# A two-layer mLSTM/gMLP trunk on one core: the opening phase in a new order, with x transposed first and the gates last

## The chip, the cores and the metric

The kernel runs on one core of a Trainium2 chip. Its time is the device time of one execution in microseconds (us). A core has TensorE (PE, matrix products; PEld is its weight load), VectorE (DVE), ScalarE (ACT) and GpSimd (POOL), and SyncE (SP), which here only issues loads and stores. SBUF is the memory on the core, PSUM the eight banks into which TensorE writes.

## The reference

Input x is 512 rows of 1024 numbers; c is one row of 1024. There are two layers. Each has a token mixer (layer 0: mLSTM, layer 1: a chunked gMLP) and a channel MLP. Around each stands adaLN: shift, scale and gate are computed from c.

```python
mod = silu(c) @ ada_w[i] + ada_b[i]
sh1, sc1, g1, sh2, sc2, g2 = split(mod, 6)
h = rmsnorm(x, norm_g[i, 0]) * (1.0 + sc1) + sh1
y = mixer(h)                                  # layer 0: mLSTM
x = x + g1 * rmsnorm(y, norm_g[i, 1])
h = rmsnorm(x, norm_g[i, 2]) * (1.0 + sc2) + sh2
x = x + g2 * rmsnorm(square(relu(h @ ffn_w1[i])) @ ffn_w2[i], norm_g[i, 3])
```

The mLSTM mixer projects h with one matrix of 3088 columns: q (512 columns, 8 heads of 64), k (512), v (1024), o (1024), input gates (8) and forget gates (8). From the gates come, per head, running sums and running maxima along the sequence, which give decay masks for the scores q k^T in chunks of 128 rows and the state that goes from chunk to chunk. All is float32.

## The kernel before

Products of float32 matrices are done as three matmuls of rounded parts (`mm3`): each operand is split into a rounded half (hi) and the remainder (lo), and hi*hi, hi*lo and lo*hi are added in one PSUM bank. `conv` makes the two halves of a weight block: ScalarE rounds, VectorE subtracts. Weight blocks of 1 MB go through a ring of five buffers (`raw`). Each engine works through its own queue in order. In the opening, which is pinned, the order on an engine is that of the program; behind the line `pinned[0] = False` a planner orders the instructions.

The layer-0 adaLN columns are computed in eight steps, one for each 128 of the 1024 features, since step k of the projections needs shift and scale of features 128k to 128k+127. For one step, `ada_load` brings 1 MB of `ada_w` (two loads of 512 KB, shift and scale, in pieces of 512 bytes). `ada_init` lets ScalarE multiply two of its eight row groups by silu(c) into two accumulators, `ada_acc` adds the other six on VectorE, `ada_merge` adds the accumulators on POOL, `ada_tr` transposes the result on TensorE, and `ada_fin` sums along the row on VectorE and makes the two columns in three small operations.

The opening of `mlstm` (lines 531 to 645) goes like this. SP issues the load of c, the adaLN block 0, the four tiles of x (512 KB each), then four small loads of gate weights in pieces of 32 bytes, the gate biases, and from there one q block (256 KB) and one adaLN block for each step. ScalarE issues four small loads of packed vectors from its own queue, before its first computing instruction. x is normalised per row: ScalarE squares and sums, POOL takes the power -1/2, VectorE scales. In the loop over k (8 steps) TensorE transposes four blocks of normalised x into PSUM, ScalarE applies scale and shift (`feed`), rounds, and POOL subtracts; POOL also subtracts for the q weights. Then TensorE does 15 matmuls of 512 columns: three for the gates and twelve for q, into five open banks. The transposes for step k+2 stand behind the matmuls of step k. After the loop k is projected, four blocks of 24 matmuls; its weights come as two loads of 1 MB. At the same time VectorE, ScalarE and TensorE compute the chain from the gates: tanh, log-sigmoid (a long polynomial on 8 partitions), running sums, running maxima, exponentials. These go through DRAM (`dm`) and come back as broadcast loads, from which POOL and ScalarE make the masks. Then v (8 units of 24 matmuls), and then scores, masks, state and the o units are interleaved by a list.

```python
        for step in "s0 k0 o0 m0 t0 o1 s1 k1 o2 m1 t1 o3 s2 k2 o4 m2 t2 g0 o5 s3 g1 o6 m3 g2 o7 g3".split():
```

Here s0 are the scores of chunk 0, o0 the first o unit, m0 the product with the masks. `prep.step()` works at the adaLN of the next part, beside the projections. PSUM is divided: five banks for `bank()`, two for `bank2()`, one for `bank3()`.

Of the kernel before, what the change touches and what calls it, by code (L numbers as in the profile page):

```python
# [8 lines left out]
F32 = mybir.dt.float32  # L9
# [24 lines left out]
def trunk(ctx: ExitStack, tc: tile.TileContext, x, c, norm_g, ada_w, ada_b, ffn_w1, ffn_w2,  # L34
# [77 lines left out]
    pool.memset(mhalf, -0.5)  # L112

# [417 lines left out]
    def mlstm(h, prep, after):  # L531
        w = a_w_in[0]
        h = HT()
        raws = [ada_load(0, 0, 1, 0)]
# [5 lines left out]
        wgs = w.rearrange("(k p) f -> p k f", p=P)  # L540
        wg = []
        for i in range(2):
            t = A(shape=(P, 4, P))
            pool.memset(t, 0.0)
            ld.dma_start(t[:, :, 0:8], wgs[:, 4 * i:4 * i + 4, 3072:3080])
            ld.dma_start(t[:, :, 32:40], wgs[:, 4 * i:4 * i + 4, 3080:3088])
# [3 lines left out]
        ld.dma_start(bcol[0:8, :], a_b_if[0, 0:8].rearrange("(p a) -> p a", a=1))  # L550
        ld.dma_start(bcol[32:40, :], a_b_if[0, 8:16].rearrange("(p a) -> p a", a=1))

        accs_ = {}
        qr = [None] * KC

        def load_q(k):
            qr[k] = A()
            ld.dma_start(qr[k], w[k * P:(k + 1) * P, 0:S])

        def ada_start(k):  # L560
            accs_[k] = R().rearrange("p (c i f) -> p c (i f)", c=2, i=2)
            ada_init(raws[k], accs_[k])

        load_q(0)
        raws.append(ada_load(0, 0, 1, 1))
        load_q(1)
        ada_start(0)
        ada_acc(raws[0], accs_[0], range(6))
        pt = bank2()
        for i in range(2):  # L570
            pe.transpose(out=pt[:, i * P:(i + 1) * P], in_=pk[:, i, :], identity=ident)
        aps = ada_tr(accs_[0])
        xn = []
        for t in range(NT):
            s = meansq(xt[t], D)
            v = small(1)
            pool.tensor_scalar_add(v, s, EPS)
            r = small(1)
            pool.tensor_tensor(out=r, in0=v, in1=mhalf[:, 0:1], op=ALU.pow)
            xs = [A(), A()]  # L580
            for s in range(2):
                dve.tensor_scalar_mul(xs[s], xt[t][:, s * S:(s + 1) * S], r)
            xn.append(xs)
            if t == 2:
                dve.tensor_copy(cols, pt[:, 0:2 * P].rearrange("p (a b) -> p a b", a=2))
                ab = [ada_fin(aps, 0, 0, 1, 0, 0)]
        accs = [bank() for _ in range(5)]
        qw = [None] * KC

        def xT(k):  # L590
            ps = bank2()
            for t in range(NT):
                pe.transpose(out=ps[:, t * P:(t + 1) * P],
                             in_=xn[t][k // 4][:, (k % 4) * P:(k % 4 + 1) * P], identity=ident)
            return ps

        def q_hi(k):
            qw[k] = A(F32R), A(F32R)
            act.copy(qw[k][0], qr[k])

        def q_lo(k):
            pool.tensor_sub(qw[k][1], qr[k], f32(qw[k][0]))

        def feed(k, ps, eng):
            full = T()
            act.activation(full, ps, AF.Identity, scale=ab[k][0], bias=ab[k][1])
            hh, hl = h(k, slice(0, S))
            act.copy(hh, full)
            eng.tensor_sub(hl, full, f32(hh))

        wgc = [conv(wg[i], lo_eng=pool) for i in range(2)]
        q_hi(0)
        q_lo(0)
        feed(0, xT(0), dve)
        pool.tensor_scalar_mul(bcol, bcol, 1.0 / CAP)
        ada_start(1)
        ada_acc(raws[1], accs_[1], range(6))
        raws.append(ada_load(0, 0, 1, 2))
        load_q(2)
        ada_start(2)  # L620
        aps = ada_tr(accs_[1])
        xps = xT(1)
        for k in range(KC):
            if k + 2 < KC:
                ada_acc(raws[k + 2], accs_[k + 2], range(6))
            if k + 1 < KC:
                ab.append(ada_fin(aps, 0, 0, 1, 0, k + 1))
            if k + 3 < KC:
                raws.append(ada_load(0, 0, 1, k + 3))
                load_q(k + 3)  # L630
                ada_start(k + 3)
            if k + 2 < KC:
                ada_merge(accs_[k + 2])
            if k + 1 < KC:
                feed(k + 1, xps, pool)
                q_hi(k + 1)
                q_lo(k + 1)
            hh, hl = h(k, slice(0, S))
# [521 lines left out]
```

## Time and profile before

| | |
|---|---|
| three timed runs | 1268.44, 1270.19, 1271.1 us; median 1270.19 |
| the profiled execution | 1269.99 us, of which the span is 1268.2 |
| PE | 1210.4 us busy, 95% of the span |
| DVE | 848.0, 67% |
| ACT | 619.5, 49% |
| POOL | 129.2, 10% |
| loads and stores | 174.24 MB, mean 137 GB/s |

The span runs from the first to the last instruction. A busy time is the time in which an engine has an instruction running. PE is almost always busy, so what ends the idle time of PE is what counts. The profile names every instruction by its engine and its tiles: `ps`, `pt`, `pa` are PSUM banks, `hhi` and `hlo` the halves of h, `whi` and `wlo` those of a weight block, `raw` a loaded block, `a` a general buffer, `r` an adaLN accumulator, `t` a short-lived buffer, `s` a small column.

### The profile page before, as it was taken

Reading aid. Unit: us, or ns where it says so; the run is one execution under the profiler, and the core shown is the slowest. Engines: PE = TensorE matmul, PEld = TensorE weight load, DVE = VectorE, ACT = ScalarE, POOL = GpSimd, SP = SyncE. Lnnn points to the kernel's source line nnn. Section 1 sums busy time; section 2 is a strip of 40 time slices with the busy share of each in tenths; the row PEclk is TensorE's granted clock in tenths of the full one; section 3 lists DMA queues with packets and bytes.
Section 4 is the critical chain, followed back from the end, with each engine's and each line's share of the span. In section 5 each row is a group of like instructions: output and inputs, shape, how many; then the busy total and the mean of one; then the engine's idle time right before and its main releaser. Section 6 shows DMA issues by size and latency. Waiting matters only on the chain.

```text
span 1268.2 us, 15234 instructions
## 1 busy us (share of the span) xinstructions
PE 1210.4 (95%) x5705; PEld 986.0 (78%) x5705; DVE 848.0 (67%) x1360; ACT 619.5 (49%) x1107; POOL 129.2 (10%) x158
## 2 busy tenths in 40 slices
PE   2999998999999999999899999999999999999997
PEld 1678777888787887778678788888798888887886
DVE  5897677573967869866666756532747758668545
ACT  4545535285555545553653644322664554545432
POOL 4601211010000000010110023300100000000000
PEclk9999999999999999999999999999999999999999
DMA  9957942433354363365256644332443332331401
GB/s 262 307 185 193 264 127 89 141 125 103 105 166 133 101 198 111 93 213 176 97 154 212 206 119 137 128 108 67 133 133 108 109 125 66 122 111 51 148 1 67
DMA packets 165722, 174.24 MB, mean 137 GB/s; under 512 B 6152, under 2 KB 121080, under 8 KB 165648
## 3 DMA queue, kind: packets, MB, share of 16 engines
q1 hardware_dynamic: 165408, 173.17, 44.0%
q8 instruction: 45, 0.74, 0.2%
q14 instruction: 29, 0.24, 0.1%
q10 hardware_dynamic: 240, 0.09, 0.0%
HBM read 171.11 MB, written 2.14 MB: 137 GB/s over the span
## 4 chain that ended last, share of the span: by engine, by line
PE 70%; DVE 11%; DMA 7%; ACT 5%; issue 2%; POOL 2%; SPq 2%; DVEq 0%; POOLq 0%; ACTq 0%
PE ps L50 49%; PE pt L50 21%; DMA raw<-in_ada_w 5%; DVE wlo L50 3%; DVE a L50 3%; DVE r L50 2%; SPq L50 2%; ACT whi L50 2%; ACT j L50 2%; POOL s L50 1%; ACT t L50 1%; DMA a<-in_b_ws 1%; DVE x L50 1%; DMA raw<-in_a_w_in 1%; DVE s L50 1%
## 5 line engine op out<-in xcount | busy, mean ns | idle before, releaser
L50 DVE TENSOR_TENSOR wlo<-raw,whi 128x1024 fp32r<-128x1024 f32 x232 | 284.8, 1232 | 203.0 <-ACT whi L50 197.5
L50 PE MATMUL ps<-whi,a 128*128 128x512 f32 x1312 | 418.9, 394 | 0.5 <-DVE a L50 0.3
L50 ACT CAST whi<-raw 128x1024 fp32r<-128x1024 f32 x232 | 242.4, 1051 | 309.6 <-PE ps L50 220.4
L50 PEld LDWEIGHTS ps<-whi,a 128*128 128x128 f32 x1312 | 246.4, 188 | 61.8 <-DVE a L50 5.4
L50 PE MATMUL ps<-wlo,a 128*128 128x512 f32 x656 | 256.7, 392 | 0.0
L50 DVE SCALAR_TENSOR_TENSOR r<-raw,cact,r 128x256 f32<-128x256 f32 (+1 forms) x256 | 143.7, 599 | 26.1 <-ACT r L50 13.3
L50 PE MATMUL pt<-hhi,whi 128*128 128x512 f32 x384 | 150.7, 392 | 2.2 <-ACT t L50 1.3
L50 PE MATMUL pt<-hhi,wlo 128*128 128x512 f32 x384 | 149.9, 391 | 1.5 <-DVE wlo L50 1.5
L50 PE MATMUL pt<-hlo,whi 128*128 128x512 f32 x384 | 149.5, 389 | 0.0
L50 PEld LDWEIGHTS ps<-wlo,a 128*128 128x128 f32 x656 | 123.6, 188 | 25.3 <-DVE wlo L50 1.2
L50 PE MATMUL ps<-hlo,whi 128*128 128x512 f32 (+1 forms) x360 | 127.7, 355 | 2.4 <-POOL hlo L50 2.4
L50 PE MATMUL ps<-hhi,whi 128*128 128x512 f32 (+1 forms) x360 | 129.1, 359 | 0.3 <-ACT whi L50 0.3
L50 PE MATMUL ps<-hhi,wlo 128*128 128x512 f32 (+1 forms) x360 | 127.5, 354 | 0.7 <-DVE wlo L50 0.7
L50 DVE TENSOR_TENSOR a<-a,a 128x512 fp32r<-128x512 f32 (+2 forms) x162 | 105.1, 685 | 32.0 <-ACT a L50 31.7
L50 PE MATMUL ps<-wlo,hhi 128*128 128x512 f32 x256 | 102.6, 401 | 6.0 <-DVE wlo L50 5.8
L50 PE MATMUL ps<-whi,hhi 128*128 128x512 f32 x256 | 102.7, 402 | 2.1 <-ACT whi L50 2.1
L50 PE MATMUL ps<-whi,hlo 128*128 128x512 f32 x256 | 101.5, 396 | 0.0
L50 ACT CAST a<-a 128x512 fp32r<-128x512 f32 x108 | 63.2, 616 | 53.9 <-POOL a L50 41.8
L50 POOL TENSOR_TENSOR s<-s,mhalf 128x1 f32<-128x1 f32 (+1 forms) x40 | 32.4, 811 | 548.9 <-DVE s L50 541.6
L50 PEld LDWEIGHTS pt<-hhi,whi 128*128 128x128 f32 x384 | 72.1, 188 | 19.0 <-ACT whi L50 2.5
L50 PEld LDWEIGHTS pt<-hhi,wlo 128*128 128x128 f32 x384 | 72.1, 188 | 18.6 <-DVE wlo L50 3.7
L50 PEld LDWEIGHTS pt<-hlo,whi 128*128 128x128 f32 x384 | 72.1, 188 | 14.7
(128 smaller groups left out, 1376.8 us busy)
## 6 DMA issues: line engine op xcount, KB each, us to landing
raw<-in_ffn_w SPq DMA_DIRECT2D x64, 1024.0 KB, 5.1
raw<-in_ada_w SPq DMA_DIRECT2D x64, 512.0 KB, 5.5
raw<-in_ada_w SPq DMA_DIRECT2D x16, 1024.0 KB, 5.1
raw<-in_b_w_in SPq DMA_DIRECT2D x16, 1024.0 KB
raw<-in_a_w_in SPq DMA_DIRECT2D x10, 1024.0 KB, 10.2
raw<-in_b_w_out SPq DMA_DIRECT2D x8, 1024.0 KB, 5.0
raw<-in_a_w_out SPq DMA_DIRECT2D x4, 1024.0 KB, 5.0
x<-in_x SPq DMA_DIRECT2D x4, 512.0 KB, 6.5
```

The source lines that it names most:

```text
L50: r = f(*a, **k)
```

## The change

The opening of `mlstm` is written anew; the rest of the kernel, but for the small column function, stays.

SP now loads x first, and then for each step the adaLN block, the q block and 384 of the 512 columns of k, 192 KB. Steps 0 to 2 are loaded at once, step k+3 behind the matmuls of step k. x is normalised, transposed by TensorE (32 blocks) and copied by ScalarE and VectorE into two of the five `raw` buffers before the loop. ScalarE starts one accumulator from one row group (`init`), VectorE adds seven (`sums`), and the sum over partitions is a product with a column of ones on TensorE (`total`), which gives a column at once. The column operations become two (`ada_cols`), as 1 is added to all scale biases once. The remainders of weights and of h are made by VectorE, no longer by POOL. The loop does 21 matmuls per step, for q (four banks) and three quarters of k (three banks). The gates come behind the loop, 24 matmuls; their weights come by one load in the third step and are spread by POOL. The last quarter of k is one block of 24 matmuls.

```diff
-        ab = cp.tile([P, 4], F32, tag="ab", name=nm("ab"), bufs=16)
-        dve.tensor_scalar(ab[:, 2:3], s[:, 1:2], abcol(l, vc, k), 1.0, ALU.add, ALU.add)
+        return ada_cols(s, l, vs, vc, ng, k)
+
+    def ada_cols(s, l, vs, vc, ng, k):
+
+        ab = cp.tile([P, 2], F32, tag="ab", name=nm("ab"), bufs=16)
+        dve.tensor_scalar(ab[:, 1:2], s[:, 1:2], abcol(l, vc, k), ngcol(l, ng, k), ALU.add, ALU.mult)
         dve.tensor_add(ab[:, 0:1], s[:, 0:1], abcol(l, vs, k))
-        dve.tensor_mul(ab[:, 1:2], ab[:, 2:3], ngcol(l, ng, k))
...
+        QK = S + 3 * P
+        def load(k):
+            raws[k] = ada_load(0, 0, 1, k)
+            raw = A(), A()[:, 0:QK - S]
+            ld.dma_start(raw[0], w[k * P:(k + 1) * P, 0:S])
+            ld.dma_start(raw[1], w[k * P:(k + 1) * P, S:QK])
+            qk[k] = [raw]
...
+        def init(k):
+            accs_[k] = R()[:, 0:2 * P]
+            act.activation(accs_[k], flat(k, KC - 1), AF.Copy, scale=cact[:, KC - 1:KC])
+        def sums(k):
+            a = accs_[k]
+            for j in range(KC - 1):
+                dve.scalar_tensor_tensor(out=a, in0=flat(k, j), scalar=cact[:, j:j + 1], in1=a,
+                                         op0=ALU.mult, op1=ALU.add)
+        def total(k):
+            ps = bank3()
+            for i in range(2):
+                pe.matmul(ps[:, i:i + 1], lhsT=accs_[k][:, i * P:(i + 1) * P], rhs=one, start=True, stop=True)
+            return ps
...
+        for k in range(3):
+            load(k)
+        xT = [rp.tile([P, 4, S], F32, tag="raw", name=nm("raw")) for _ in range(2)]
...
+        x_stat(0)
+        x_stat(1)
+        x_turn(0)
+        x_stat(2)
+        x_turn(1)
+        x_out(0)
+        x_stat(3)
+        x_turn(2)
+        x_out(1)
...
+        x_turn(3)
+        x_out(2)
+        init(0)
...
+        x_out(3)
+        sums(0)
+        sp0 = total(0)
+        ab = [ada_cols(sp0, 0, 0, 1, 0, 0)]
...
+        qk_hi(0)
+        full = feed_hi(0)
+        qk_lo(0)
+        feed_lo(0, full)
+        init(1)
+        sums(1)
+        qk_hi(1)
+        accs = [bank() for _ in range(5)] + [bank2() for _ in range(2)]
...
+        for k in range(KC):
+            main(k, range(5))
+            if k + 1 < KC:
+                sp1 = total(k + 1)
+            main(k, range(5, 7))
+            if k + 3 < KC:
+                load(k + 3)
...
+            if k + 2 < KC:
+                init(k + 2)
+            if k + 1 < KC:
+                ab.append(ada_cols(sp1, 0, 0, 1, 0, k + 1))
+                qk_lo(k + 1)
+                full = feed_hi(k + 1)
+                feed_lo(k + 1, full)
+            if k + 2 < KC:
+                qk_hi(k + 2)
+                sums(k + 2)
+        wgc = [conv(wg[i]) for i in range(2)]
+        gps = bank3()
...
+            mm3(gps, wgc[k // 4][0][:, k % 4], wgc[k // 4][1][:, k % 4], hh, hl, k == 0, k == KC - 1)
...
-        for f0 in (512, 768):
-            for blk in (kblk if f0 == 512 else w_cols(w, f0)):
-                ps = bank()
-                proj_fm(ps, blk, h, slice(0, S))
-                kk = A()
-                act.activation(kk, ps, AF.Copy, scale=DK ** -0.5)
-                kT.append(kk)
+        raw = rp.tile([P, KC, P], F32, tag="raw", name=nm("raw"))
+        ld.dma_start(raw, w[:, QK:2 * S].rearrange("(k p) f -> p k f", p=P))
+        ps = bank()
+        proj_fm(ps, conv(raw), h, slice(0, S))
+        for f in range(4):
+            kk = A()
+            act.activation(kk, accs[4 + f] if f < 3 else ps, AF.Copy, scale=DK ** -0.5)
+            kT.append(kk)
```

## Rows read from the trace of the kernel before

**Rows 1.** Busy time by stretch: from:to and length in us, then for each engine busy us and its number of instructions, the granted clock, the share of the DMA engines and GB/s. The stretches are the opening, the loop over k, the k projections, the v projections and the start of the attention part.

```profile
0.00:28.00 28.00, 4.39 (x15) 2.78 (x16) 15.65 (x33) 11.61 (x21) 12.76 (x29) 1.00 0.91 256
28.00:67.20 39.20, 36.31 (x159) 27.25 (x158) 32.74 (x64) 22.46 (x38) 24.05 (x21) 1.00 0.94 277
67.20:89.00 21.80, 21.80 (x98) 18.06 (x97) 20.55 (x27) 7.66 (x12) 0.00 (x0) 1.00 0.61 205
89.00:136.50 47.50, 47.28 (x216) 37.98 (x215) 33.82 (x70) 25.14 (x68) 8.24 (x24) 1.00 0.76 215
136.50:200.00 63.50, 57.58 (x374) 46.20 (x373) 48.25 (x148) 28.24 (x80) 11.17 (x8) 0.97 0.60 176
```

**Rows 2.** Timeline of the opening: load issues by SP and ACT and ScalarE's first computing instruction (start us, duration us, engine, operation, tiles, count), and behind them, from the view of the loads of x, the time from issue to landing.

```profile
1.27 1.03 SPq L50 DMA_DIRECT2D raw<-in_ada_w  x2
2.34 2.70 SPq L50 DMA_DIRECT2D x<-in_x  x4
2.80 0.55 ACTq L50 DMA_DIRECT2D a<-in_norm_g  x1
5.28 0.52 ACTq L50 DMA_DIRECT2D a<-in_a_hnorm_g  x1
7.17 0.38 SPq L50 DMA_DIRECT2D a<-in_a_w_in  x1
8.92 0.32 ACTq L50 DMA_DIRECT2D a<-in_b_b_in  x1
9.35 0.91 ACT L50 ACTIVATE r<-raw,cact 128x256 f32<-128x256 f32 x2 [6.38 <-DMA x<-in_x]
12.82 0.37 SPq L50 DMA_DIRECT2D a<-in_a_w_in  x1
...
DMA to landing us min/median/max: 6.5/6.5/6.5
```

**Rows 3.** Timeline: the steps by which x is made ready, and the first products of adaLN on VectorE.

```profile
9.89 2.46 DVE L50 SCALAR_TENSOR_TENSOR r<-raw,cact,r 128x256 f32<-128x256 f32 x6 [5.77 <-DMA a<-in_a_hnorm_g]
10.16 1.04 ACT L50 ACTIVATE j<-x 128x1024 bf16<-128x1024 f32 x1
13.57 0.57 POOL L50 TENSOR_TENSOR s<-s,mhalf 128x1 f32<-128x1 f32 x1
14.18 0.88 DVE L50 TENSOR_SCALAR a<-x,s 128x512 f32<-128x512 f32 x2 [1.82 <-POOL s L50]
37.83 0.60 PE L50 MATMUL pt<-ident,a 128*128 128x128 f32 x4
```

**Rows 4.** Timeline: the first projection, and single steps of the loop over k and their like elsewhere (h's remainder on VectorE, h scaled and rounded on ScalarE, TensorE waiting for POOL, the adaLN products beside POOL's work and without it, a column operation, f32 matmuls).

```profile
22.91 0.69 DVE L50 TENSOR_TENSOR hlo<-t,hhi 128x512 fp32r<-128x512 f32 x1 [0.63 <-ACT hhi L50]
28.03 0.78 PE L50 MATMUL ps<-hhi,whi 128*128 128x512 f32 x1
41.20 0.78 ACT L50 ACTIVATE t<-pt,ab 128x512 f32<-128x512 f32 x1 [1.87 <-DVE ab L50]
42.01 0.62 ACT L50 CAST hhi<-t 128x512 fp32r<-128x512 f32 x1
44.26 0.51 PE L50 MATMUL ps<-hlo,whi 128*128 128x512 f32 x1 [1.07 <-POOL hlo L50]
45.64 5.09 DVE L50 SCALAR_TENSOR_TENSOR r<-raw,cact,r 128x256 f32<-128x256 f32 x6
93.05 1.04 PE L50 MATMUL pt<-triu,s 128*8 128x128 f32 x8
144.02 0.15 DVE L50 TENSOR_TENSOR ab<-s,cols 128x1 f32<-128x1 f32 x1
147.08 3.25 DVE L50 SCALAR_TENSOR_TENSOR r<-raw,cact,r 128x256 f32<-128x256 f32 x8
```

**Rows 5.** Busy time by stretch, columns as in rows 1: TensorE's first matmuls, a stretch of the loop with a wait for POOL, and the matmuls behind the first wait for o weights.

```profile
28.00:32.00 4.00, 4.00 (x11) 3.16 (x10) 3.61 (x12) 2.15 (x5) 0.73 (x1) 1.00 1.17 305
42.70:46.00 3.30, 2.00 (x7) 1.14 (x7) 3.26 (x7) 1.54 (x4) 3.29 (x3) 1.00 1.18 300
141.40:144.60 3.20, 3.20 (x9) 2.42 (x9) 3.20 (x7) 3.18 (x7) 0.00 (x0) 0.50 0.70 205
```

**Rows 6.** Timeline of PE: the first matmul of the k projections, and the first of the v projections, 96 matmuls later.

```profile
67.18 0.39 PE L50 MATMUL ps<-hhi,whi 128*128 128x512 f32 x1
88.94 0.39 PE L50 MATMUL ps<-whi,hhi 128*128 128x512 f32 x1
```

**Rows 7.** Timeline of the chain behind the gates: tanh, the copy of the packed rows, the exponentials of the masks, the load of o weights behind the broadcast loads, and the first product of a mask with the scores.

```profile
64.42 0.68 ACT L50 ACTIVATE a<-ps,bcol 40x512 f32<-40x512 f32 x1
110.16 0.56 DVE L50 COPY a<-pt 128x384 f32<-128x384 f32 x1 [0.81 <-PE pt L50]
122.45 4.80 ACT L50 ACTIVATE a<-a,a 128x128 f32<-128x128 f32 x16 [2.27 <-POOL a L50]
122.97 1.41 SPq L50 DMA_DIRECT2D raw<-in_a_w_in  x1
144.09 0.68 DVE L50 TENSOR_TENSOR a<-a,ps 128x512 f32<-128x512 f32 x1
```

**Rows 8.** Timeline of PE in the first o block: matmuls that waited for o weights (in brackets the idle time and what ended it).

```profile
139.34 0.50 PE L50 MATMUL ps<-whi,hhi 128*128 128x512 f32 x1 [0.87 <-ACT whi L50]
147.22 0.50 PE L50 MATMUL ps<-wlo,hhi 128*128 128x512 f32 x1 [0.61 <-DVE wlo L50]
```

More of the change, by code (lines that the diff above doesn't have):

```diff
@@ L112, in trunk @@
     pool.memset(mhalf, -0.5)
+    one = cp.tile([P, 1], F32, name="one")
+    pool.memset(one, 1.0)
     ck = cp.tile([8, P], F32, name="ck")
@@ new lines, in qk_lo, with flat @@
+        def qk_lo(k):
+            raw, hi = qk[k]
+            lo = wp.tile([P, QK], F32R, tag="wlo", name=nm("wlo"))
+            dve.tensor_sub(lo[:, 0:S], raw[0], f32(hi[:, 0:S]))
+            dve.tensor_sub(lo[:, S:QK], raw[1], f32(hi[:, S:QK]))
+            qk[k].append(lo)
+        def flat(k, j):
+            return raws[k][:, j].rearrange("p a b -> p (a b)")
+        def init(k):
+            accs_[k] = R()[:, 0:2 * P]
+            act.activation(accs_[k], flat(k, KC - 1), AF.Copy, scale=cact[:, KC - 1:KC])
@@ new lines, in mlstm, with x_stat, x_turn @@
+        xT = [rp.tile([P, 4, S], F32, tag="raw", name=nm("raw")) for _ in range(2)]
+        rs, xps = {}, {}
+        def x_stat(t):
+            v = small(1)
+            pool.tensor_scalar_add(v, meansq(xt[t], D), EPS)
+            rs[t] = small(1)
+            pool.tensor_tensor(out=rs[t], in0=v, in1=mhalf[:, 0:1], op=ALU.pow)
+        def x_turn(t):
+            for s in range(2):
+                xn = A()
+                dve.tensor_scalar_mul(xn, xt[t][:, s * S:(s + 1) * S], rs[t])
+                ps = bank()
+                for j in range(4):
+                    pe.transpose(out=ps[:, j * P:(j + 1) * P], in_=xn[:, j * P:(j + 1) * P], identity=ident)
+                xps[t, s] = ps
@@ new lines, in x_out @@
+        def x_out(t):
+            for s, f in ((0, act.copy), (1, dve.tensor_copy)):
+                f(xT[s][:, :, t * P:(t + 1) * P], xps[t, s].rearrange("p (a b) -> p a b", a=4))
+        x_stat(0)
[7 more added lines that the diff above has]
+        x_out(1)
+        pt = bank2()
+        for i in range(2):
+            pe.transpose(out=pt[:, i * P:(i + 1) * P], in_=pk[:, i, :], identity=ident)
+        x_turn(3)
@@ new lines, in mlstm, with feed_hi @@
+        x_out(2)
+        init(0)
+        dve.tensor_copy(cols, pt[:, 0:2 * P].rearrange("p (a b) -> p a b", a=2))
+        scales = cols[:, 1, 0:96].rearrange("p (a b) -> p a b", b=KC)[:, 1::3, :]
+        dve.tensor_scalar_add(scales, scales, 1.0)
+        x_out(3)
+        sums(0)
+        sp0 = total(0)
+        ab = [ada_cols(sp0, 0, 0, 1, 0, 0)]
+        def feed_hi(k):
+            full = T()
+            act.activation(full, xT[k // 4][:, k % 4], AF.Identity, scale=ab[k][0], bias=ab[k][1])
+            act.copy(h(k, slice(0, S))[0], full)
+            return full
@@ new lines, in feed_lo, with main @@
+        def feed_lo(k, full):
+            hh, hl = h(k, slice(0, S))
+            dve.tensor_sub(hl, full, f32(hh))
+        qk_hi(0)
[6 more added lines that the diff above has]
+        accs = [bank() for _ in range(5)] + [bank2() for _ in range(2)]
+        def main(k, fs):
+            hh, hl = h(k, slice(0, S))
+            for f in fs:
+                cs = slice(f * P, (f + 1) * P)
+                mm3(accs[f], qk[k][1][:, cs], qk[k][2][:, cs], hh, hl, k == 0, k == KC - 1)
@@ L541, in mlstm @@
+        wgr = A()[:, 0:KC * 2 * NH].rearrange("p (k f) -> p k f", k=KC)
         wg = []
@@ L565, in mlstm @@
[L565 to L602, printed above, removed]
@@ L647, in mlstm @@
+        wgc = [conv(wg[i]) for i in range(2)]
+        gps = bank3()
+        for k in range(KC):
+            hh, hl = h(k, slice(0, S))
+            mm3(gps, wgc[k // 4][0][:, k % 4], wgc[k // 4][1][:, k % 4], hh, hl, k == 0, k == KC - 1)
         pinned[0] = False
```

77 lines of the change are left out of this document (19 added, 58 removed).

## The prediction, made before the changed kernel was timed

> **What bounds the kernel now.** I read the busy time by stage first. The reader should see one bound nearly everywhere: from the first projections on, TensorE is busy 36.3 of 39.2 us, then all of 21.8, then 47.3 of 47.5 [rows 1]. The exception is the opening. In the first 28 us TensorE works 4.4 us, while loads move 256 GB/s, and the attention part that starts at 136.5 us loses about 6 us more [rows 1]. So the change can win only where TensorE waits now: before the first projection at 28.03 [rows 4], inside the loop over k, and indirectly in the attention part, whose start depends on the forget-gate chain.
>
> Next I read the timeline of the opening [rows 2], to see what the first projection waits for: loads, then ScalarE, then VectorE. After that comes one turn of the loop with the durations of its steps [rows 3, 4], then the chain behind the gates [rows 7] and the waits of the first o block [rows 8].
>
> All sums go against the profiled execution: 1269.99 us, of which the span is 1268.2. That is 0.2 us under the median of the three timed runs, 1270.19.
>
> **Part 1, up to the first projection.** ScalarE is the gate. It issues four small loads from its own queue, and its first computing instruction waits behind them: the fourth goes out at 8.92 and takes 0.32, and at 9.35 ScalarE begins [rows 2]. The issue times tell why. Counted from the load of c, the tenth load goes out at 5.28, the eleventh at 7.17 and the twelfth at 8.92. The fourth (x, issued 2.34, landing after 6.5) lands at 8.84 [rows 2]. I read it so: about eight loads are under way at once, and the next waits for the oldest. By the same reading the load at 12.82 waited for the last tile of x, so tiles of x land (12.82 - 8.84) / 3 = 1.3 us apart and halves of the adaLN block 1.9 apart [rows 2].
>
> In the new order the SP queue begins c, four of x, two of adaLN, q, k. The first lands as the adaLN half did, at about 5.3 [rows 2]; x is complete at 5.3 + 3 x 1.3 = 9.2, the adaLN halves follow at 11.1 and 13.0, q and k by some 14.6. Which places ScalarE's four loads get is not shown. If they come right behind c, ScalarE is free by 8; if each alternates with an SP load that waits as well, the fourth is the seventeenth and waits for the ninth, until 14.6. I take the middle, the thirteenth or fourteenth place, behind x's last tile or adaLN's first half: about 10.
>
> From there, the chain by rows: four statistics (1.04 each, put at 1.2 with the reading of the sum) with a copy of 0.6 between them, so that the fourth ends some 5.2 us after the start; 1.05 for POOL's add and power (0.57 for the power, the rest an estimate); 0.9 for two scalings; 0.6 for four transposes; VectorE's copies, cols and scales about 1.6; seven products of adaLN at 0.41, 2.9; ones-column sums 0.4; two column operations 0.3; scaling and rounding of h 0.7 + 0.62 [rows 3, 4]. With hops this is 14.2 until the rounded half of h is there and 15.0 until the remainder is. So the first matmul comes at 24.2, and they run freely from 25.0, against 28.03 before: 3.0 us earlier. Bounds by the ends of ScalarE's wait: 5 earlier to 1.6 later.
>
> **Part 2, the loop.** TensorE's matmuls are 0.2267 apart (96 from 67.18 to 88.94 [rows 6]). The count of big matmuls is the same, 216, but they move: 168 in the loop, then 24 for the gates and 24 for the last quarter of k. The six transposes of each turn leave, and two sums by a ones column come. They are f32 matmuls; the nearest row takes 1.04 for four with 128 columns, written as eight instructions [rows 4]. Two with one column I put at 0.4, between 0.3 and 0.6.
>
> A turn is now a ring: sums on TensorE 0.4; two column operations 0.3; h scaled 0.7 (0.78 from PSUM before); rounded 0.62; remainder on VectorE 0.69; hops 0.2; then the fourteen matmuls that need the remainder and stand ahead of the next sums, 3.2. That is 6.1 us. Only the last six matmuls (1.4 us) run beside the 2.5 us of feeding, so TensorE waits about 1.1 each turn. VectorE has 0.3 + 1.2 (the weights' remainders, which leave POOL) + 0.7 + 2.9 = 5.1 and fits, because POOL is quiet. The products took 5.09 for six beside POOL's subtractions and 3.25 for eight without them [rows 4]; at the dear price VectorE would set the turn, at 7.4. The floor is TensorE's own 21 matmuls and sums, 5.2. I take 6.1. ScalarE needs 2.9 a turn. Loads need 1.44 MB, 5.2 us at the 277 GB/s of the loop before [rows 1], and run three turns ahead, so they are covered; without that lead the turn would still be 6.1. The adaLN buffers fall from five to three, since two hold the transposed x, but the one that turn k frees was summed three turns before.
>
> The first turn starts slowly. From 28 to 32 eleven matmuls took 4 us, with a spacing of the lower level, though the clock column says 1.00 there [rows 5]. The same happens again, since TensorE idles before it: nine matmuls at 0.43 and six at 0.23 make 5.2 us. So: 25.0 + 5.2 + 0.4 + 2.5 = 33.1 for the second turn, + 6 x 6.1 = 69.7 for the eighth, + 20 x 0.2267 = 74.2, + 48 x 0.2267 = 85.1 for the end of k. Before it was 88.94 [rows 6]. The gain is 3.8 us.
>
> **Part 3, what moves to nothing.** The gate weights' small loads leave SP's front (7.17 to 13.2 [rows 2]) for the third turn, where SP runs ahead. The POOL copies of them at the fifth turn have three turns to finish; uncovered they cost about 2 us once. The three later weight blocks of k vanish from the stretch behind the loop. One column operation fewer in each later adaLN step lies under matmuls. The seven banks are freed by copies that can run under the gates' matmuls; if they came late, 1 us.
>
> **Part 4, the gates.** Here something is paid. The gates' result was ready at 64.42, 24.5 us ahead of the v projections; now it comes 5.4 ahead of them, at about 79.9, 15.5 later. From tanh to the copy of the packed rows took 45.7, and the exponentials began at 122.45 [rows 7]; the first pair ends 2.4 later at 124.8. Shifted by 15.5 that is 140.3. The product that needs them came at 144.09 [rows 7], 7.6 behind the end of v; with v ending 3.8 earlier it could come at 140.3. So it just fits, if the chain is not longer. It should be shorter, since VectorE has three weight blocks fewer and idles at the loop's end. I charge 0; bounds: 3.9 better (the two waits of the first o block [rows 8], a third of about 0.8 and the 1.6 of its matmuls at half clock [rows 5] disappear) and 15.5 + 3.8 worse (everything shifts with the gates).
>
> Sum: 1269.99 - 3.8 = 1266.2.
>
> **Rivals.** (a) ScalarE is held to 14.6: the first projection then starts at 28.8, k ends 4.6 later than forecast, at 89.7, 0.8 behind before: 1270.8. For it: SP always has loads ready to take the places. Against it: ScalarE's loads stand earlier in the program. A turn of 6.7 instead of 6.1 gives the same.
>
> (b) Slower, by one mechanism: the weights of the first o block queue on SP behind the sixteen broadcast loads that wait for the gates. The second of them went out at 122.97, straight behind those [rows 7], and its remainder ended TensorE's wait at 147.22 [rows 8]. If the order stays, this issue moves with the gates by up to 15.5. It decides as soon as the shift exceeds the 3.8 gained plus the wait there is now. Half the shift, since the chain gets shorter, gives 1269.99 + 7.7 = 1277.7; all of it 1285.5. Against it: the buffers that these weights need come free earlier than the gates, so they may be placed first.
>
> (c) Early loads and no stall at the o block: 2.5 (ScalarE free at 7.5) and up to 3.9 more on top of 3.8: 1259.8.
>
> (d) The clock. In the loop before, TensorE waited over 1 us for POOL at 44.26 [rows 4], and the stretch around it shows 1.00 granted [rows 5]; behind the waits at the o block it fell to 0.50, the 1.2 GHz level [rows 5]. If the waits of every turn drop it so, 21 matmuls at 0.43 cost 4.2 more in seven turns: 1296. The Trainium skill (TensorE: Matmul & The Clock Gate, "HAM oscillation — how this bites in real kernels") says that a loop over K whose every step ends in a wait for operands can begin each step again at the low clock. By that rule it is this 1296; the trace agrees at the o block and not in the loop, so I give it little.
>
> **Chances.** Forecast 0.44 (its own range 1262.5 to 1269), (a) 0.21, (b) 0.19, (c) 0.13, (d) 0.03. The range 1259 to 1278 leaves out (d), half of (b) and the best part of (c), under 0.2. A difference below 0.2%, 2.5 us, can't be told from none here. Faster: 0.44 x 0.85 + 0.13 = 0.50. Same: 0.44 x 0.15 + 0.21 x 0.8 = 0.24. Slower: the rest of (a), (b), (d), 0.26.
>
> **What would show it.** In the profile after: ScalarE's first statistic near 10 (8 to 14.6 tells Part 1); the first 512-column matmul near 24; turns 6.1 apart, with waits for the rounded h and its remainder and no drop of the clock; the end of k near 85; tanh near 80; the masks' exponentials before 141; no wait on o weights longer than 1.4. The prediction is wrong if VectorE, not the feeding ring, sets the turn, if ScalarE is still issuing loads at 13, or if the first o block waits for weights that were issued behind the broadcast loads.

## The result, and the profile after

The changed kernel takes 1285.61 us (1281.27 to 1288.71) where the kernel before takes 1269.32 (1268.0 to 1271.1): a ratio of 1.0125, 95% interval 1.0091 to 1.016. It is 16.3 us slower, and the prediction of 1266.2 was wrong. The profiled execution took 1286.98 us, its span 1285.3. In the page, PE is now busy 1219.9 us (1210.4 before), DVE 850.9, ACT 618.7 and POOL 99.8 (129.2 before).

The busy times by stretch, with the columns of [rows 1], say where the time went:

```profile
0.00:28.00 28.00, 10.67 (x47) 8.85 (x48) 15.59 (x35) 12.82 (x23) 7.33 (x24) 0.87 1.02 293
28.00:67.20 39.20, 35.40 (x144) 24.86 (x142) 28.96 (x66) 15.19 (x27) 1.98 (x6) 0.96 0.73 203
67.20:89.00 21.80, 18.68 (x78) 14.08 (x79) 18.28 (x28) 10.58 (x17) 0.00 (x0) 1.00 0.79 278
89.00:136.50 47.50, 40.92 (x183) 32.69 (x182) 41.23 (x76) 17.78 (x39) 4.68 (x17) 0.93 0.68 202
136.50:200.00 63.50, 55.41 (x320) 45.23 (x319) 37.10 (x105) 30.66 (x90) 10.08 (x12) 0.95 0.52 141
```

The opening is better, as forecast. From 67 us on every stretch has fewer PE instructions than in [rows 1]: 78 for 98, 183 for 216, 320 for 374. The largest hole lies in the v projections, where TensorE had been busy 47.3 of 47.5 us and is now busy 40.9.

The timeline of the opening (columns as in [rows 2]) answers Part 1: ScalarE's fourth load, its first statistic, the first products, the first sums by the ones column, the first projection.

```profile
7.57 0.32 ACTq L50 DMA_DIRECT2D a<-in_b_b_in  x1
7.94 1.06 ACT L50 ACTIVATE j<-x 128x1024 bf16<-128x1024 f32 x1 [5.15 <-DMA x<-in_x]
17.70 3.60 DVE L50 SCALAR_TENSOR_TENSOR r<-raw,cact,r 128x256 f32<-128x256 f32 x7
21.35 1.02 PE L50 MATMUL pa<-one,r 128*128 128x1 f32 x4 [4.53 <-DVE r L50]
24.36 0.79 PE L50 MATMUL ps<-hhi,whi 128*128 128x512 f32 x1 [2.00 <-ACT hhi L50]
```

One turn of the loop, from the remainder of h to the next one:

```profile
40.23 0.69 DVE L50 TENSOR_TENSOR hlo<-t,hhi 128x512 fp32r<-128x512 f32 x1 [0.47 <-ACT hhi L50]
40.84 3.60 DVE L50 SCALAR_TENSOR_TENSOR r<-raw,cact,r 128x256 f32<-128x256 f32 x7
44.49 0.61 PE L50 MATMUL pa<-one,r 128*128 128x1 f32 x4
45.14 0.28 DVE L50 TENSOR_SCALAR ab<-pa,cols 128x1 f32<-128x1 f32 x1 [0.70 <-PE pa L50]
45.52 0.82 ACT L50 ACTIVATE t<-raw,ab 128x512 f32<-128x512 f32 x1 [3.98 <-DVE ab L50]
46.37 0.62 ACT L50 CAST hhi<-t 128x512 fp32r<-128x512 f32 x1
47.04 0.49 PE L50 MATMUL ps<-hhi,whi 128*128 128x512 f32 x1 [0.43 <-ACT hhi L50]
47.02 0.69 DVE L50 TENSOR_TENSOR hlo<-t,hhi 128x512 fp32r<-128x512 f32 x1 [0.47 <-ACT hhi L50]
```

Read it as a ring. From 40.23 to 47.02 is 6.79 us: remainder, seven products, sums, column operations, scaling, rounding, remainder. The eighth turn begins at 74.20.

Behind the loop come tanh, the copies that free the q banks, the copies of v out of their banks, TensorE's waits, and the first matmul of the o block:

```profile
86.00 0.68 ACT L50 ACTIVATE a<-pa,bcol 40x512 f32<-40x512 f32 x1
86.58 2.01 ACT L50 COPY a<-ps 128x512 f32<-128x512 f32 x4
92.80 0.39 PE L50 MATMUL ps<-whi,hhi 128*128 128x512 f32 x1
122.17 0.40 PE L50 MATMUL ps<-whi,hlo 128*128 128x512 f32 x1
125.19 0.44 PE L50 MATMUL pa<-ident,r 128*128 128x128 f32 x2 [2.17 <-POOL r L50]
130.04 1.76 PE L50 MATMUL pt<-ident,a 96*128 96x96 f32 x8 [4.41 <-ACT a L50]
130.01 2.86 ACT L50 COPY a<-ps 128x384 f32<-128x384 f32 x10
131.12 0.54 DVE L50 COPY a<-pt 128x384 f32<-128x384 f32 x1
131.45 0.78 PE L50 MATMUL ps<-whi,hhi 128*128 128x512 f32 x1
156.79 0.80 PE L50 MATMUL ps<-whi,hhi 128*128 128x512 f32 x1 [5.21 <-ACT whi L50]
```

v begins at 92.80 (88.94 in [rows 6]). The matmul at 122.17 is the 120th of v, and the 121st starts only at 131.45: between them stand in TensorE's queue an adaLN transpose, which waits 2.17 for POOL, and the transposes of the packed rows, which wait 4.41 for the gate chain. From tanh to the copy of the packed rows the chain takes 45.1 us, as before (45.7 in [rows 7]). Then the o block, which began at 139.34 [rows 8], waits 5.21 for its weights and begins at 156.79. From there on the gap stays at 15 to 18 us: the first load of the mixer's output weights (`a_w_out`) goes out 14.9 us later than before (193.81 for 178.94), and the span is 17.1 longer.

The row at 130.01 points at the cause, though I did not see it at first. ScalarE copies v out of its banks only then, ten copies in one go. In the kernel before, the same view has

```profile
110.50 1.74 ACT L50 COPY a<-ps 128x384 f32<-128x384 f32 x6
114.09 0.65 ACT L50 COPY a<-ps 128x384 f32<-128x384 f32 x2
119.10 0.39 PE L50 MATMUL ps<-whi,hlo 128*128 128x512 f32 x1
```

The copies stand right behind the packed rows' copy at 110.16 [rows 7]; the matmul at 119.10 is the 120th of v, and the 121st follows it 0.23 later. v has five banks, and five banks are 120 matmuls: 27.2 us at the spacing of [rows 6], and by the traces 29.4 to 31.4, since other work of TensorE stands between them. Before, the fifth bank was full at 119.3, and the copies came 8.8 earlier. After, it is full at 122.4, and the copies come 7.6 later.

### The profile page after: what moved, and what is told of

It reads as the page before. It is cut to its first block, busy times and chain, and to the rows that moved or that the text cites. A ratio compares the mean times of both kernels' runs of the same rounds, so it can differ in the third digit from the quotient of the medians.

```text
span 1285.3 us, 15218 instructions
## 1 busy us (share of the span) xinstructions
PE 1219.9 (95%) x5721; PEld 990.6 (77%) x5721; DVE 850.9 (66%) x1355; ACT 618.7 (48%) x1108; POOL 99.8 (8%) x138
## 4 chain that ended last, share of the span: by engine, by line
PE 69%; DVE 13%; ACT 6%; DMA 6%; issue 4%; POOL 2%; SPq 0%; POOLq 0%; DVEq 0%; ACTq 0%
PE ps L50 47%; PE pt L50 21%; DMA raw<-in_ada_w 4%; DVE r L50 4%; DVE a L50 3%; DVE wlo L50 3%; ACT t L50 2%; ACT whi L50 2%; ACT j L50 1%; POOL s L50 1%; PE pa L50 1%; ACT a L50 1%; DMA a<-in_b_ws 1%; DVE x L50 1%; DVE s L50 1%
## 5 line engine op out<-in xcount | busy, mean ns | idle before, releaser
L50 DVE TENSOR_TENSOR wlo<-raw,whi 128x1024 fp32r<-128x1024 f32 x229 | 280.2, 1228 | 204.1 <-ACT whi L50 196.7
L50 ACT CAST whi<-raw 128x1024 fp32r<-128x1024 f32 x229 | 239.2, 1051 | 309.7 <-PE ps L50 213.6
L50 PE MATMUL pt<-hhi,whi 128*128 128x512 f32 x400 | 157.6, 394 | 2.2 <-ACT t L50 1.3
L50 PE MATMUL pt<-hhi,wlo 128*128 128x512 f32 x400 | 156.2, 391 | 1.1 <-DVE wlo L50 1.1
L50 PE MATMUL pt<-hlo,whi 128*128 128x512 f32 x400 | 155.8, 389 | 0.0
L50 PE MATMUL ps<-hhi,whi 128*128 128x512 f32 (+1 forms) x368 | 133.5, 363 | 7.1 <-ACT hhi L50 5.1
L50 PE MATMUL ps<-hlo,whi 128*128 128x512 f32 (+1 forms) x368 | 132.4, 360 | 1.6 <-DVE hlo L50 1.6
L50 PE MATMUL ps<-hhi,wlo 128*128 128x512 f32 (+1 forms) x368 | 131.6, 358 | 1.4 <-DVE s L50 0.7
L50 PEld LDWEIGHTS ps<-hhi,whi 128*128 128x128 f32 x368 | 70.2, 191 | 19.7 <-ACT hhi L50 8.2
L50 ACT CAST a<-a 128x512 fp32r<-128x512 f32 x100 | 58.2, 616 | 53.6 <-POOL a L50 42.1
```

What stands on the lines that cost most here:

```text
L50: r = f(*a, **k)
```

## The experiments

All times are medians, and each ratio is against the kernel before on the same chip. That kernel's median lies between 1267.8 and 1270.3 in the groups of runs, so a difference in us between two groups is uncertain by some 2 us.

**1. Gates earlier.** The gates' matmuls move from behind the eighth turn to ahead of its matmuls.

```diff
+            if k == KC - 1:
+                gps = bank3()
+                for j in range(KC):
+                    gate(j)
             main(k, range(5))
...
+            if k == KC - 2:
+                wgc = [conv(wg[i]) for i in range(2)]
```

> The changed kernel with the gates' 24 matmuls moved ahead of the eighth turn of the loop (steps 0 to 6 fill TensorE's wait there), the rest alike. Theory G (the late gates cost the time: the chain behind tanh runs as long as before, 45 us, and TensorE's and ScalarE's queues stand behind it): tanh near 79 instead of 86.0, so the waits of 2.2 and 4.4 us before the packed rows' transposes and most of the 5.2 us before the first o block go; 1272 to 1276. Rival L (the slower loop alone costs it): the waits stay or move, and only the filled wait of some 1 to 3 us is won; 1283 to 1285.

Measured: 1277.1, ratio 1.0069 (1.0046 to 1.0092). tanh starts at 79.07, the packed copy at 125.02. Some half of the loss is gone: 9.3 us are left, a little more than theory G gave, since TensorE still waits 3.03 and 1.95 ahead of the packed rows and 2.46 at the o block.

**2. Two accumulators.** The products alternate between two halves of the accumulator; one addition joins them.

```diff
-            for j in range(KC - 1):
+            for j in range(KC - 2):
+                a = accs_[k][:, j % 2]
...
+            dve.tensor_add(accs_[k][:, 0], accs_[k][:, 0], accs_[k][:, 1])
```

> The changed kernel with two adaLN accumulators that take turns, six products and one addition on VectorE instead of seven products into one, ScalarE starting both. Theory A (a product that reads what the one just before it wrote costs 0.52 instead of 0.41): the sums of one step take 2.9 instead of 3.6 us, turns fall from 6.8 to about 6.3, the last k block ends some 3 us earlier and the whole is 2 to 4 us faster than the changed kernel (1282 to 1284). Rival (VectorE's products are slow for another reason, such as loads that write beside them): 0.5 each stays, turns stay at 6.8 and the time at 1286.

Measured: 1282.76, ratio 1.0111 (1.009 to 1.0133). The turn falls to 6.5, the eighth begins at 70.89 (74.20 in the changed kernel). Six products take 2.46, 0.41 each again, as in [rows 4]: theory A holds.

**3. q copies first.** ScalarE copies the q banks ahead of the tanh instead of behind it, in the part whose order is that of the program.

```diff
-        pinned[0] = False
         qT, kT = [], []
...
         for f in range(4):
             q = A()
             act.copy(q, accs[f])
             qT.append(q)
+        pinned[0] = False
+
+        gt = A()
+        act.activation(gt[0:40], gps[0:40], AF.Tanh, scale=1.0 / CAP, bias=bcol[0:40])
```

> The changed kernel with the four copies of q placed ahead of tanh in ScalarE's queue, so that the last k block's bank is free when the gates end. Both theories: the 2.0 us wait of TensorE at 85 is gone. Theory G (the chain behind the gates sets the end of this part): tanh is not earlier, the won 2 us come back as a longer wait behind it; 1285 to 1287. Rival (TensorE's waits add up): 1283 to 1284.

Measured: 1281.12, ratio 1.0098 (1.0076 to 1.012). Both theories missed. The wait of 1.96 is gone, v begins at 89.55, 3.25 earlier, and the time gains 4.5, or 3.0 with each kernel held against its own kernel before. The masks' exponentials follow the packed copy by 11.2 us here and by 14.1 in the changed kernel.

**4. The old opening with late gates.** In the kernel before, the gates' matmuls move out of the loop and behind three blocks of k. With them the q copies go ahead of the tanh, and the three blocks of k into the part whose order is that of the program. Nothing of the new opening is in it.

```diff
-            mm3(accs[0], wgc[k // 4][0][:, k % 4], wgc[k // 4][1][:, k % 4], hh, hl, k == 0, k == KC - 1)
...
+        for blk in kblk[:3]:
+            k_proj(blk)
+        for k in range(KC):
+            hh, hl = h(k, slice(0, S))
+            mm3(accs[0], wgc[k // 4][0][:, k % 4], wgc[k // 4][1][:, k % 4], hh, hl, k == 0, k == KC - 1)
```

> The kernel before, with its opening and loop, but the 24 matmuls of the gates taken out of the loop and put behind three of the four k blocks. The same number of matmuls. Theory G: tanh moves from 64.4 to about 84, the transposes of the packed rows come when TensorE has no other work ahead of them, and the time rises to 1278 to 1285. Rival L: the opening and the loop are as before, so 1268 to 1272.

Measured: 1284.47, ratio 1.0122 (1.0097 to 1.0146). tanh starts at 90.90. This edit costs as much as the whole change, but not all of it in Part 4: v begins at 95.42, 6.5 later than before, mostly since in the loop TensorE now waits 4.9 us for POOL's share of the operands (0.4 before) without the gates' matmuls to fill the time. What is paid behind the start of v is 9 us. Theory L falls.

**5. All three edits together.**

> The changed kernel with all three edits that each gained alone: the gates' matmuls ahead of the eighth turn's, two accumulators for the sums, and the copies of q ahead of the tanh. Theory G (time follows how late the gates' result comes): the eighth turn starts at about 71.6 as with two accumulators alone, so tanh starts near 76.5, 3 to 9 us earlier than in any of the three, and the time is 1270 to 1275. Rival S (the three gains are separate and add): 8.5 + 2.8 + 4.5 below 1285.6, which is 1269 to 1271, whatever tanh does. Rival M (one wait hides behind the other, the largest single gain is all there is): 1276 to 1278.

Measured: 1278.77, ratio 1.0077 (1.0062 to 1.0092): no earlier than experiment 1 alone, and near rival M's range. tanh starts at 78.60, and TensorE waits 2.55 and 4.42 us ahead of the packed rows, more than with the first edit alone (3.03 and 1.95): v begins 2.9 earlier, at 85.40, and the packed copy only 0.8 earlier. Theories G and S fall: an earlier end of k brought nothing.

**6 and 7. No filler.** VectorE serves the chain in turn with steps of the next layer's adaLN. These eight steps leave the loop over v in the changed kernel and, as a control, in the kernel before; they are done later.

```diff
                     hd += n
-                prep.step()
```

> The changed kernel without the eight steps of the next layer's adaLN work in the loop over v (they are done later, from the o loop on; nothing is left out). Theory V (the chain from tanh to the packed rows is 45 us long because VectorE serves it in turn with these steps): the chain falls from 45.1 to 28 to 35 us, the packed copy comes at 114 to 121 instead of 131.1, TensorE's waits of 2.2, 4.4 and 5.2 us between 120 and 160 go, and the time falls to 1270 to 1277. Rival L (the chain's own steps and their hops set its length): it stays above 40, time 1284 to 1287. Rival M (the steps cost as much in the o loop): the chain is shorter and the time still above 1282, with new waits after 160.

> The kernel before without the same eight steps in its loop over v: what moving them does by itself where the gates are early. Theory V: there the packed copy at 110.2 had room to spare, so an earlier one brings little: 1265 to 1269, against 1267.8. Rival M (the steps cost where they are put): 1270 to 1276.

Measured: 1288.66 (ratio 1.0154, 1.0137 to 1.0171) and 1282.47 (1.011, 1.0093 to 1.0128). In the control the chain from tanh (64.37) to the packed copy (104.90) falls from 45.7 to 40.5, and the time still rises by 12.6, more than either side gave. The filler is a ninth of the chain, and the steps cost where they are put: between 140 and 330 us TensorE now waits 8.8 us for POOL's additions of adaLN, where the kernel before shows no such wait. Theory V falls.

**8. Gates in the loop.** Two steps of the gates per turn in turns five to eight, in place of one of the three banks of k, whose quarter goes behind the loop; the gate weights are loaded and spread two turns earlier. The edits of 2 and 3 are in it too.

```diff
-        QK = S + 3 * P
+        QK = S + 2 * P
...
+            if k >= 4:
+                gate(2 * k - 8)
+                gate(2 * k - 7)
             main(k, range(5))
```

> The changed kernel with two accumulators and q's copies first, and the gates' 24 matmuls spread over turns five to eight (two steps of k each, ahead of the turn's own), in place of a quarter of k, which goes behind the loop with the last: six open banks for q and half of k, one for the gates. Theory G: the eighth turn starts near 72, tanh near 74, the end of k near 88, and the time is 1268 to 1273, for the gates are still 9 us later than before. Rival E (only the end of k counts): 1266 to 1268.

Measured: 1269.52, ratio 0.9997 (0.998 to 1.0014). The time is where theory G put it, but not for its reason: tanh starts at 78.90, no earlier than in experiment 5, because it stands behind the q copies, and the time is 9 us shorter. So not the gates' lateness by itself is paid. Here the packed copy (120.69) comes 3.0 us behind the fifth bank (90.45 + 27.2), and TensorE waits 0.20 for it.

With this I set the runs so far side by side. "Late" is the packed copy minus the time at which v's fifth bank would be full without other work between (first v matmul + 27.2; by the traces it is full 2.3 to 4.3 later in each run); "hole" is the time from the 120th v matmul to the 121st; "excess" is the time above the kernel before (1269.0, the middle of its medians of 1267.8 to 1270.3) minus the shift of the first v matmul against 88.94.

| run | first v matmul | packed copy | late | hole | time | excess |
|---|---|---|---|---|---|---|
| before | 88.94 | 110.16 | -6.0 | 0.2 | 1269.0 | 0 |
| changed | 92.80 | 131.12 | 11.1 | 9.3 | 1285.6 | 12.7 |
| gates earlier | 88.34 | 125.02 | 9.5 | 7.9 | 1277.1 | 8.7 |
| two accumulators | 89.47 | 127.79 | 11.1 | 9.3 | 1282.8 | 13.3 |
| q copies first | 89.55 | 128.47 | 11.7 | 9.7 | 1281.1 | 11.5 |
| old opening, late gates | 95.42 | 132.60 | 10.0 | 8.4 | 1284.5 | 9.0 |
| all three | 85.40 | 124.23 | 11.6 | 9.7 | 1278.8 | 13.3 |
| gates in the loop | 90.45 | 120.69 | 3.0 | 0.2 | 1269.5 | -1.0 |

The excess goes with the lateness behind the banks, not with the tanh. The place of the hole says the same: in each of the six kernels that lose behind v's start it lies exactly behind the 120th matmul, whatever else differs, and the two without a loss have none. In the changed kernel v's last matmuls come 8.4 later behind its first than before, and the o block's wait is 4.3 longer (5.21 for 0.87); together these are the 12.7. That the banks are the cause was theory B, and the next runs put it to the test.

**9 and 10. v tiles early.** The twelve buffers that v is copied into are asked for behind the tanh and the q copies, ahead of the chain's own buffers from the same pool of forty, instead of behind the chain; in the changed kernel, and in the kernel before as a control.

```diff
         act.activation(gt[0:40], gps[0:40], AF.Tanh, scale=1.0 / CAP, bias=bcol[0:40])
...
+        vt = [[A(shape=(P, 3, DV + 1)) for _ in range(3)] for _ in range(NT)]
+        for n in range(NT):
+            for j in range(3):
+                pool.memset(vt[n][j][:, :, DV:DV + 1], 1.0)
         fg = A()[0:8]
```

> The changed kernel with one thing moved: the twelve tiles that take v (and the ones in their last column) are asked for ahead of the gate chain's own tiles, behind the tanh; the gates stay where the change put them. Theory B (banks): in the changed kernel ScalarE copies the first five banks of v at 130.01, right behind the chain's last exponentials, since the tiles for v come free only with the chain's; five banks are 120 matmuls, and TensorE stands with all five full. With the tiles asked for earlier the copies come as the banks fill, the waits of 2.17 and 4.41 us before 135 go, v ends near 139 instead of 148.7, the first o matmul comes before 143 instead of 156.8, and the time falls to 1271 to 1276, though tanh stays at 86. Rival C (the late chain itself is what costs, through the masks' exponentials and the weight casts behind them on ScalarE): tanh unchanged, so the wait for the cast stays and the time is above 1281.

> The kernel before with the same move, as a control. Theory B: there the copies of v come at 110.5, before the fifth bank is full (88.94 + 27.2 = 116.1), so no wait is there to be removed: 1267 to 1271. If asking for the tiles earlier is worth something by itself: 1262 to 1266.

Measured: 1274.24 (ratio 1.0044, 1.0027 to 1.006) and 1269.21 (1.0003, 0.9993 to 1.0013). 11.1 of the 16.3 us are gone, though the packed copy comes only 1.9 earlier, at 129.24; where nothing waited for the banks, the same move is worth nothing. The timeline of the changed kernel with this move shows the copies of v, the packed rows' transposes, and the first o matmul:

```profile
98.83 0.65 ACT L50 COPY a<-ps 128x384 f32<-128x384 f32 x2 [2.66 <-PE ps L50]
104.27 0.65 ACT L50 COPY a<-ps 128x384 f32<-128x384 f32 x2 [4.79 <-PE ps L50]
128.68 0.52 PE L50 MATMUL pt<-ident,a 96*128 96x96 f32 x4 [0.50 <-ACT a L50]
137.06 1.06 ACT L50 CAST whi<-raw 128x1024 fp32r<-128x1024 f32 x1 [0.15 <-PE ps L50]
142.76 0.48 PE L50 MATMUL ps<-whi,hhi 128*128 128x512 f32 x1
147.27 4.78 ACT L50 ACTIVATE a<-a,a 128x128 f32<-128x128 f32 x16
```

These copies wait for TensorE's bank alone; the 121st v matmul follows the 120th 0.22 later, and TensorE waits 0.50 for the chain where it waited 4.41; the wait of 2.17 for POOL ahead of it is gone too. The second half follows from the first: v ends earlier, so ScalarE casts three of the four o weight blocks ahead of the masks' exponentials, and the o block starts at 142.76 instead of 156.79. Of the 5.2 us that are left, 4.2 are the later start of v (93.19).

**11. All three edits with v tiles early.**

> The run with all three edits (gates ahead of the eighth turn's matmuls, two accumulators, q copies first; 1278.8) and the v tiles asked for early. Theory B: its waits of 2.55, 4.42 and 3.95 us before the o block go, k ends near 87.5, 1.4 before that of the kernel before, and the time is 1266 to 1270. Rival C: its tanh at 78.6 is 14 us later than before, and the time stays above 1274.

Measured: 1266.16, ratio 0.9985 (0.9976 to 0.9995). Against experiment 5 the one move brings 12.6 us (11.8 with each held against its own kernel before); tanh (79.19) is still 14.8 later than before, and the kernel is level with before or a little faster. Rival C falls.

**12. A steady VectorE.** The gates of 1, the accumulators of 2, v tiles early, and two of the six products of the sums after next behind this turn's sums. The cut shows the edit against the kernel of 2.

```diff
-        def sums(k):
-            for j in range(KC - 2):
+        def sums(k, js=range(KC - 2)):
+            for j in js:
...
+                sums(k + 2, range(2, KC - 2))
+            if k + 3 < KC:
+                init(k + 3)
+                sums(k + 3, (0, 1))
```

> Gates ahead of the eighth turn's matmuls, two accumulators, v tiles early, and two of the six products of the sums after next put behind this turn's sums, so that VectorE works while TensorE adds up the sums and ScalarE feeds h. Theory: the turn was a ring with about 1.2 us in which VectorE idles; filled, the turn falls from 6.5 to 5.5 to 5.9, the eighth turn starts near 67, k ends near 83, and the time is 1261 to 1266. Rival (the hops of the ring count, not the products): the turn stays above 6.3 and the time is 1266 to 1270.

Measured: 1269.21, ratio 0.9995 (0.9982 to 1.0008). The turn stays at 6.5. That is what the rival gave, but neither side had named why: the sums stand in TensorE's queue behind fourteen matmuls, as the next two runs show.

**13 and 14. The sums sooner.** In the kernel of 11 the sums stand behind three banks' matmuls of a turn instead of five; then the same with the products brought forward as in 12, from the second turn on.

```diff
-            main(k, range(5))
+            main(k, range(3))
             if k + 1 < KC:
                 sp1 = total(k + 1)
-            main(k, range(5, 7))
+            main(k, range(3, 7))
```

> The kernel of the run with all three edits and early v tiles (1266.2; turn 6.5), with one thing moved: TensorE adds up the next sums behind three of the seven banks' matmuls of a turn instead of five. Theory R (the ring runs over TensorE's queue: fourteen matmuls behind the remainder of h, 3.2 us, stand ahead of the sums): with eight ahead, 1.8 us, the products (six and the merge, 2.9 us behind the remainder) end later than these and set the ring, so the turn falls only by about 0.3, to 6.2, and the time to 1263.5 to 1265.5. Rival P (VectorE's products set it already): turn 6.5 and 1265 to 1268.

> The same with two of the six products of the sums after next put behind this turn's sums on VectorE, as in the run with a steady VectorE, from the second turn on. Theory R: the sums are now complete 2.1 us behind the remainder of h, about when the eighth matmul ends, and the turn falls to 5.5 to 5.8, the eighth turn starts near 66.5, k ends near 81.5, and the time is 1260 to 1264. Rival P: VectorE is the bound (5.6 us of work a turn and the wait for the rounded h), turn 6.0 to 6.3 and 1263 to 1266. Rival C: k ends earlier, but the masks' exponentials, which follow the tanh, end the wait at the o block, and the time stays at 1266.

Measured: 1264.71 (ratio 0.9951, 0.9933 to 0.997) and 1260.34 (0.9918, 0.9903 to 0.9932). The turns are 6.1 and 5.3. In the first kernel's timeline of PE, the sums wait for VectorE's products in every turn but the first, for example:

```profile
46.86 0.61 PE L50 MATMUL pa<-one,r 128*128 128x1 f32 x4 [0.62 <-DVE r L50]
52.97 0.61 PE L50 MATMUL pa<-one,r 128*128 128x1 f32 x4 [0.61 <-DVE r L50]
```

In the second kernel's no wait is left from the third turn on:

```profile
51.49 0.55 PE L50 MATMUL pa<-one,r 128*128 128x1 f32 x4
56.81 0.56 PE L50 MATMUL pa<-one,r 128*128 128x1 f32 x4
62.12 0.57 PE L50 MATMUL pa<-one,r 128*128 128x1 f32 x4
```

The second kernel beats both: 0.8% under the kernel before, 2% under the changed one. Theory R holds, and the rest of the kernel follows the end of k to within 2 us in the runs 11, 13 and 14, where v's banks are free in time.

## Why the prediction was wrong, and where it was right

**Part 1 held, by two errors that cancel.** The first matmul came at 24.36 and the second at 25.09, forecast 24.2 and 25.0. ScalarE was free at 7.94 instead of about 10, at the early end of the range given, and the chain behind it took 16.4 us instead of 14.2: among others the seven products took 3.60, not 2.9, and the first ones-column sums 1.02, not 0.4.

**Part 2: the mechanism was right, two terms were mis-sized.** The ring was the right picture, but "fourteen matmuls, 3.2" was not its longest link. Beside them run the seven products, which I had priced at 0.41 from a row with two accumulators in turn [rows 4]; the new `sums` adds all seven into one, and they come 0.52 apart: 3.60. So the sign of error that the prediction had named, VectorE setting the turn, came true in this form: not by its whole work (5.41 of 6.80 us busy), but as a link of the ring. With the sums 0.65 instead of 0.4 (to the column operation's start), the turn is 0.61 + 3.65 + 0.65 + 0.38 + 0.85 + 0.65 = 6.79, and not 6.1. Experiment 2 gives the first correction (6.5, now set by the fourteen matmuls), 13 and 14 the rest (6.1 set by the products, 5.3 by TensorE itself, near the floor of 5.2 that I gave). Six turns at 0.7 make 4.1 us. Two side sums of this part were off without weight in the result: at the dear price seven products make VectorE's turn 8.1, not 7.4, and the loads of a turn are 1.51 MB (1472 KB), 5.4 us.

**Part 3: one edit was not free.** "If they came late, 1 us" was 1.96: the q copies stand behind the tanh, and the tanh behind a cast. With that, the 4.1 of the turns, and 1.1 for the second turn's remainder (34.2, forecast 33.1), 7.2 of the 7.7 us by which k ends later than forecast (92.8, not 85.1) are accounted for.

**Part 4 failed, and it is the step that made the sign wrong.** "I charge 0" rested on one due time, the first product with the scores at 144.09. The chain has an earlier customer. The copies of v stood right behind it at 110.50, and v's five banks were full at 119.3; so the chain could come about 9 us later, not 15.5, before TensorE had to stand (some 13 with v itself 3.9 later). It came 21 later. I had not asked who else waits for the chain's end, since in the trace of before nobody did: the copies came with room to spare, and a wait that is not there has no row. "It should be shorter" hardly came true: 45.1 against 45.7. The 12.7 of excess in the table are inside the worse bound I gave (15.5 + 3.8), with the wrong place: not the product with the masks, but PSUM banks and two queues served in order.

**The rivals.** (b) had the size by luck: all of a shift of 15.5 gives 1285.5, against 1285.6 measured, but the gates came 21.6 later. Its place was wrong. The second load of weights for the first o block went out at 117.73, ahead of the broadcast loads (the one at 130.03 is for the second block), so SP did not hold it; ScalarE held the cast, behind the exponentials:

```profile
117.73 0.37 SPq L50 DMA_DIRECT2D raw<-in_a_w_in  x1
130.70 15.34 SPq L50 DMA_DIRECT2D a<-dm  x16
152.13 3.67 ACT L50 ACTIVATE a<-a,a 128x128 f32<-128x128 f32 x12
155.71 3.87 ACT L50 CAST whi<-raw 128x1024 fp32r<-128x1024 f32 x4
```

(a) did not happen at the start, but its "turn of 6.7" did. Of (c) one half came true, ScalarE free early; the stall at the o block did not go away. (d) did not happen: in the loop TensorE waits 0.43 and 0.23 in every turn, and the stretch from 40.2 to 47.0 shows 1.00 granted. Around the long waits behind v it fell:

```profile
40.20:47.00 6.80, 6.11 (x25) 4.23 (x25) 5.41 (x12) 2.79 (x6) 0.73 (x4) 1.00 0.87 230
121.50:131.40 9.90, 3.32 (x17) 2.47 (x16) 9.85 (x28) 5.50 (x13) 1.98 (x2) 0.74 0.93 240
156.80:160.00 3.20, 3.20 (x13) 3.01 (x14) 3.20 (x3) 3.20 (x5) 0.00 (x0) 0.50 0.00 0
```

Those are stretches of the changed kernel with the columns of [rows 1]. The low level (0.50, 1.2 GHz) adds a little behind each long wait (at 132 two matmuls are 0.43 apart, at 133.5 they are 0.23); it is a consequence of the waits. The rule of the Trainium skill that the prediction weighed (TensorE: Matmul & The Clock Gate, "HAM oscillation — how this bites in real kernels") speaks of a loop whose matmuls in each step are shorter than the wait for the next operands. The waits of 0.43 and 0.23 in a turn of 6.79 are no such case, so these runs do not test it.

**What stays open.** Which of the chain's buffers held the copies of v was not tried, nor whether it was a buffer alone or also the copies' place in ScalarE's queue; the runs show only that asking for v's buffers first lets the copies come early. Nor was it tried to move the packed rows' transposes in TensorE's queue by themselves; that the hole lies behind the 120th matmul in six kernels speaks against their place as the cause, but is no experiment.

## What to carry to other kernels

When a step is moved later, list everything that is released by its end, buffers of a shared pool and PSUM banks included, and take the earliest due time, not the one on the visible chain; a release that came with room to spare shows no wait, so look for work that starts just behind the step's end. For a loop that is a ring, write down both what is queued ahead of each link and the links in series, and price a chain of operations into one accumulator by a row with one accumulator.

## What the runs showed of the hardware that I had not expected

Products on VectorE (128x256, f32) that add into one accumulator start 0.52 us apart with POOL quiet (seven in 3.60); the same products in turn into two accumulators start 0.40 apart (six in 2.46, from experiment 2):

```profile
38.94 2.46 DVE L50 SCALAR_TENSOR_TENSOR r<-raw,cact,r 128x256 f32<-128x256 f32 x6
```

One product by itself has the same length in both, 0.48. So here a product that needs the result of the one before it starts 0.1 us later, behind that one's end and not ahead of it. The Trainium skill (VectorE: DVE Perf Modes, "The DRAIN you can't avoid") says that the next operation does not start until the pipe has emptied, and that one that is not held starts earlier. The trace agrees with the first for the single accumulator and with the second for the two, and adds the price.
